# RMSNorm with Silu on one core: from six slots of four rows a partition to three slots of eight

## The chip, the cores and the metric

The kernel runs on one core of a Trainium2 chip. The time is device microseconds of one execution, the median of several runs. Beside it there is a profiled execution, with its span from the first to the last instruction, and a trace that lists instructions and DMA packets. The core's engines are called PE (TensorE, matrix products), DVE (VectorE), ACT (ScalarE), POOL (GpSimd) and SP (SyncE, which here only issues DMAs). Data moves between HBM and the on-chip memory SBUF by 16 DMA engines. SyncE and ScalarE each have a queue of DMAs; both queues are served by the same 16 engines.

## What is computed

The input x has 8 x 1024 rows of 2048 float32 values, 67.1 MB; the output is as large. Each row is divided by its root mean square, multiplied by gamma, and put through Silu.

```python
def reference(x, gamma, eps):
    rms = np.sqrt(np.mean(x ** 2, axis=-1, keepdims=True) + eps)
    out = gamma * x / rms
    return (out * (1 / (1 + np.exp(-out)))).astype(np.float32)
```

## The kernel before

The 8192 rows are cut into 16 blocks of 512. In a block each of the 128 partitions holds J = 4 rows that follow one another in HBM, so that a partition's share is one run of 4 x 8 KB = 32 KB, and a block is 4 MB. A pool has BUFS = 6 slots of one block each (192 KB a partition in all). A block is computed in place and stored from its slot, and then the slot is free for the sixth block after it.

For one block b the steps are:

- `load(b)`: one DMA of the block, issued on ScalarE's queue (L54).
- `squares_scalar(b)` and `squares_vector(b)`: for each row the sum of squares, on ScalarE by an activation Square with an accumulator (L65), on VectorE by a multiply with an accumulator (L73). `share(b)` says how many rows ScalarE takes: two, or one for the even blocks from 4 to 12. What the squares write goes to PSUM tiles `junk_a` and `junk_v` that nobody reads.
- `root(b)`: the square root of the mean plus eps, on ScalarE (L82). It needs another activation table than Silu, so that table loads (ACT_TABLE_LOAD) stand ahead of L82 and L98.
- `invert(b)`: the reciprocal, on VectorE (L87), which gives rstd.
- `multiply(b)`: x times rstd times gamma, row by row in one VectorE instruction with two products (L92). gamma lies in the tile `g`, spread over all partitions at the start by four matrix products with a column of ones (L113) and a copy (L115).
- `silu(b)`: Silu in place, two rows to an instruction, on ScalarE (L98), and then `store(b)`: one DMA of the block, issued on SyncE's queue (L102).

The order is written out by hand (manual_schedule): each engine runs its instructions in the order in which the program text names them, and waits only for the data, buffers and semaphores that an instruction needs. Blocks 0 to 5 are loaded at the start: 0 and 1 first, the other four after gamma's copy. From then on the load of block b + 3 is issued by ScalarE within the squares of block b + 1, behind whatever ScalarE still has to do, and it waits for the store of block b - 3. In the loop over b the steps of blocks b and b + 1 are interleaved in three ways: one for b < SOON = 3, one for the middle, one for the last two. The last block is done differently: its product is with gamma alone (L155), and rstd goes into Silu as a scale, row by row (L157).

Of the kernel before, what the change touches and what calls it, by code (L numbers as in the profile page):

```python
# [1 line left out]

# [4 lines left out]

ACT = mybir.ActivationFunctionType
ALU = mybir.AluOpType


@with_exitstack
def kernel(
    ctx: ExitStack,
    tc: tile.TileContext,
    x: bass.AP,
    gamma: bass.AP,
    eps: bass.AP,
    out: bass.AP,
):  # L20

    nc = tc.nc
    P = nc.NUM_PARTITIONS
    f32 = mybir.dt.float32
    x2 = x.flatten_outer_dims()
    o2 = out.flatten_outer_dims()  # L30
    n, d = x2.shape
    J = 4
    BUFS = 6
    nblk = n // (P * J)
    xb = x2.rearrange("(b p j) d -> b p (j d)", p=P, j=J)
    ob = o2.rearrange("(b p j) d -> b p (j d)", p=P, j=J)

    singles = ctx.enter_context(tc.tile_pool(name="singles", bufs=1))
    pool = ctx.enter_context(tc.tile_pool(name="pool", bufs=BUFS))
    small = ctx.enter_context(tc.tile_pool(name="small", bufs=2))  # L40
    psum = ctx.enter_context(tc.tile_pool(name="psum", bufs=1, space=bass.MemoryType.PSUM))

    Q = 4
    w = d // Q
    g = singles.tile([P, d], f32)
    eps_t = singles.tile([P, 1], f32)
    ones = singles.tile([P, P], f32)
    junk_a = psum.tile([P, d], f32, name="junk_a")
    junk_v = psum.tile([P, d], f32, name="junk_v")
    blocks, sss, rmss, rstds = {}, {}, {}, {}  # L50

    def load(b):
        xt = pool.tile([P, J * d], f32, name="xt")
        nc.scalar.dma_start(out=xt, in_=xb[b])  # L54
        blocks[b] = xt

    def row(b, j):
        return blocks[b][:, j * d:(j + 1) * d]

    def squares_scalar(b, loads=()):  # L60


        sss[b] = small.tile([P, J], f32, name="ss")
        for j in range(share(b)):
            nc.scalar.activation(out=junk_a, in_=row(b, j), func=ACT.Square,  # L65
                                 accum_out=sss[b][:, j:j + 1])
            if j == 0:
                for s in loads:
                    load(s)

    def squares_vector(b):
        for j in range(share(b), J):
            nc.vector.tensor_tensor_reduce(  # L73
                out=junk_v, in0=row(b, j), in1=row(b, j), scale=1.0, scalar=0.0,
                op0=ALU.mult, op1=ALU.add, accum_out=sss[b][:, j:j + 1])

    def share(b):
        return 1 if 4 <= b <= 12 and b % 2 == 0 else 2

    def root(b):  # L80
        rms = small.tile([P, J], f32, name="rms")
        nc.scalar.activation(out=rms, in_=sss.pop(b), func=ACT.Sqrt, scale=1.0 / d, bias=eps_t)  # L82
        rmss[b] = rms

    def invert(b):
        rstd = small.tile([P, J], f32, name="rstd")
        nc.vector.reciprocal(out=rstd, in_=rmss.pop(b))  # L87
        rstds[b] = rstd

    def multiply(b):  # L90
        for j in range(J):
            nc.vector.scalar_tensor_tensor(out=row(b, j), in0=row(b, j), scalar=rstds[b][:, j:j + 1],  # L92
                                           in1=g, op0=ALU.mult, op1=ALU.mult)

    def silu(b):
        for h in range(0, J, 2):
            cols = slice(h * d, (h + 2) * d)
            nc.scalar.activation(out=blocks[b][:, cols], in_=blocks[b][:, cols], func=ACT.Silu)  # L98
        store(b)

    def store(b):
        nc.sync.dma_start(out=ob[b], in_=blocks[b])  # L102

    with tc.manual_schedule():

        load(0)
        nc.vector.memset(ones, 1.0)  # L107
        nc.vector.memset(eps_t, float(eps))
        nc.scalar.activation(out=junk_a[:, 0:1], in_=ones[:, 0:1], func=ACT.Square)  # L109
        nc.sync.dma_start(out=g[0:1, :], in_=bass.AP(tensor=gamma.tensor, offset=gamma.offset, ap=[[d, 1], [1, d]]))  # L110
        for c in range(Q):
            cols = slice(c * w, (c + 1) * w)
            nc.tensor.matmul(junk_v[:, cols], ones[0:1, :], g[0:1, cols], start=True, stop=True)  # L113
        load(1)
        nc.vector.tensor_copy(out=g, in_=junk_v)  # L115
        nc.scalar.copy(out=junk_a[:, 0:1], in_=junk_v[:, d - 1:d])  # L116
        for b in range(2, BUFS):
            load(b)

        last = nblk - 1
        SOON = 3
        squares_scalar(0)
        squares_vector(0)
        root(0)
        invert(0)
        for b in range(last):
            loads = [b + 3] if BUFS <= b + 3 < nblk else []
            if b < SOON:  # L130
                multiply(b)
                squares_scalar(b + 1, loads)
                silu(b)
                squares_vector(b + 1)
                root(b + 1)
            elif b < last - 1:
                squares_scalar(b + 1, loads)
                squares_vector(b + 1)
                root(b + 1)
                multiply(b)  # L140
                silu(b)
            else:
                multiply(b)
                squares_scalar(b + 1)
                silu(b)
                squares_vector(b + 1)
                root(b + 1)
            if b + 1 < last:
                invert(b + 1)


        for j in range(J):
            if j == J // 2:
                invert(last)
            nc.vector.tensor_mul(out=row(last, j), in0=row(last, j), in1=g)  # L155
        for j in range(J):
            nc.scalar.activation(out=row(last, j), in_=row(last, j), func=ACT.Silu,  # L157
                                 scale=rstds[last][:, j:j + 1])
        store(last)


# [1 line left out]
_INS = ['x', 'gamma', 'eps']  # L163
_OUTS = [((8, 1024, 2048), 'float32')]

_NUMBERS = {'eps': 9.999999747378752e-06}


# [26 lines left out]
```

## Time and profile before

| what | value |
|---|---|
| median of 3 runs (lowest, highest) | 316.79 us (316.73, 317.04) |
| span of the profiled execution | 315.1 us |
| moved by DMA, mean rate over the span | 134.24 MB, 426 GB/s |
| DMAs: loads, stores, gamma | 16, 16, 1 |
| one 4096 KB load, median from issue to landing | 38.7 us |
| one 4096 KB store, median from issue to landing | 29.0 us |
| first store issued, last store issued | 35.2 us, 300.9 us |
| VectorE's last instruction starts | 294.2 us |
| ACT_TABLE_LOAD, each | 1283 ns, 31 times |

The page gives the busy time of each engine and how busy the 16 DMA engines are in 40 equal slices of the span. A digit is a tenth, and 9 means 90% or more. A group's line names a line of the kernel, the engine, the operation, the tiles written and read, their shape and the count; then the busy time in all and the mean of one in ns; then the idle time of the engine just before these instructions, and what ended it. A line of the waits names who waited for whom: microseconds in total, the number of times, the longest. The engine's long waits name a DMA or another engine; whether a wait matters depends on what is busy meanwhile.

The trace's packet records go deeper than the page: each packet that a DMA engine moved is listed with its queue, start, duration and bytes. Here a partition's run of 32 KB is one packet, a load is 128 packets, 8 on each of the 16 engines, and a DMA ends on each engine with a packet of 4 bytes that counts up its semaphore.

### The profile page before, as it was taken

The page shows a single profiled execution, that of the slowest core. Times are in us where ns is not written, and L with a number is a line of the kernel's source. Part 1 is how long each engine was busy: PE and PEld are TensorE (multiplying, and loading weights), DVE is VectorE, ACT ScalarE, POOL GpSimd, SP SyncE. Part 2 cuts the span into 40 slices and gives each one's busy share as a digit, 9 for nine tenths or more (in the row PEclk, how much of TensorE's full clock was granted, in tenths as well). Part 3 has the DMA queues.
Part 4 walks back from the last instruction along what each step waited for, and adds up shares of the span by engine and source line. Part 5 has one row for each costly group of instructions (what it writes and reads, how often), then busy time and mean ns, then how long its engine had stood idle before and what let it go on. Part 6 is the DMA issues. An engine that isn't in the chain of part 4 may idle for free.

```text
span 315.1 us, 439 instructions
## 1 busy us (share of the span) xinstructions
PE 7.2 (2%) x8; PEld 2.5 (1%) x8; DVE 235.3 (75%) x157; ACT 213.9 (68%) x137; POOL 0.2 (0%) x4
## 2 busy tenths in 40 slices
PE   6200000000000000000000000000000000000000
PEld 2000000000000000000000000000000000000000
DVE  0679697979895695957969489593995939999600
ACT  1269998972799258682687827877278768779910
POOL 0000000000000000000000000000000000000000
DMA  8999999999999999999999999999999999999997
GB/s 334 412 453 416 383 458 408 462 403 462 403 459 408 454 412 458 408 462 403 462 403 462 408 458 408 458 408 458 416 449 416 449 416 449 428 437 428 437 428 308
DMA packets 4613, 134.24 MB, mean 426 GB/s; under 512 B 514, under 2 KB 514, under 8 KB 514
## 3 DMA queue, kind: packets, MB, share of 16 engines
q10 hardware_dynamic: 2304, 67.11, 49.8%
q1 hardware_dynamic: 2306, 67.12, 49.3%
q14 instruction: 3, 0.02, 0.0%
HBM read 67.12 MB, written 67.11 MB: 426 GB/s over the span
## 4 chain that ended last, share of the span: by engine, by line
DMA 68%; DVE 14%; ACT 11%; issue 1%; ACTq 1%; DVEq 0%
DMA xt<-in_x_dram 68%; DVE xt L92 9%; DVE junk_v L73 5%; ACT xt L98 4%; ACT junk_a L65 3%; ACT xt L157 2%; ACT L82 1%; ACTq L190 1%; ACT L157 0%; ACT L98 0%; ACT rms L82 0%; DVE ss L73 0%; ACTq L54 0%; DVE rstd L87 0%; ACT L109 0%
## 5 line engine op out<-in xcount | busy, mean ns | idle before, releaser
L92 DVE SCALAR_TENSOR_TENSOR xt<-xt,rstd,g 128x2048 f32<-128x2048 f32 x60 | 137.0, 2346 | 0.1
L98 ACT ACTIVATE xt<-xt 128x4096 f32<-128x4096 f32 x30 | 108.3, 3615 | 27.4 <-DVE xt L92 27.4
L73 DVE CUSTOM_DVE_ANT_0 junk_v<-xt 128x2048 f32<-128x2048 f32 x37 | 85.1, 2299 | 42.9 <-DMA xt<-in_x_dram 42.2
L65 ACT ACTIVATE junk_a<-xt 128x2048 f32<-128x2048 f32 x27 | 50.7, 1876 | 16.1 <-DMA xt<-in_x_dram 14.0
L82 ACT ACT_TABLE_LOAD x15 | 19.2, 1283 | 26.6 <-DVE ss L73 26.5
L98 ACT ACT_TABLE_LOAD x14 | 18.0, 1283 | 0.2
L115 DVE COPY g<-junk_v 128x2048 f32<-128x2048 f32 x1 | 2.3, 2292 | 9.0 <-PE junk_v L113 9.0
L87 DVE RECIPROCAL rstd<-rms 128x4 f32<-128x4 f32 x16 | 2.7, 172 | 8.4 <-ACT rms L82 8.4
L155 DVE TENSOR_TENSOR xt<-xt,g 128x2048 f32<-128x2048 f32 x4 | 8.9, 2277 | 0.0
L82 ACT ACTIVATE rms<-ss,eps_t 128x4 f32<-128x4 f32 x16 | 4.8, 297 | 5.7 <-DVE ss L73 5.5
L157 ACT ACTIVATE xt<-xt,rstd 128x2048 f32<-128x2048 f32 x4 | 7.7, 1991 | 0.0
L113 PE MATMUL junk_v<-g,ones 1*128 1x512 f32 x8 | 7.2, 1072 | 2.8 <-DMA g<-in_gamma_dram 2.8
L116 ACT COPY junk_a<-junk_v 128x1 f32<-128x1 f32 x1 | 0.1, 144 | 9.8 <-DVE g L115 9.8
L73 DVE DVE_READ_ACCUMULATOR2_ANT ss<- 128x1 f32 x37 | 5.2, 141 | 0.0
L65 ACT ACTIVATION_READ_ACCUMULATOR junk_a<-xt 128x1 f32 x27 | 5.0, 186 | 0.0
L113 PEld LDWEIGHTS junk_v<-g,ones 1*128 1x128 f32 x8 | 2.5, 325 | 5.9 <-issue 5.9
L109 ACT ACT_TABLE_LOAD x1 | 1.3, 1283 | 1.1 <-PEq L176 1.1
L157 ACT ACT_TABLE_LOAD x1 | 1.3, 1283 | 0.0
L107 DVE MEMSET ones<- 128x128 f32 x1 | 0.2, 165 | 0.8 <-PEq L176 0.8
L109 ACT ACTIVATE junk_a<-ones 128x1 f32<-128x1 f32 x1 | 0.2, 174 | 0.0
L176 POOL MEMSET const-bfloat16-1.0<- 128x1 bf16 x1 | 0.1, 103 | 0.0
L176 POOL MEMSET const-uint8-127<- 128x1 uint8 x1 | 0.1, 102 | 0.0
(3 smaller groups left out, 0.3 us busy)
## 6 DMA issues: line engine op xcount, KB each, us to landing
xt<-in_x_dram ACTq DMA_DIRECT2D x16, 4096.0 KB, 38.7
out_dram<-xt SPq DMA_DIRECT2D x16, 4096.0 KB, 29.0
g<-in_gamma_dram SPq DMA_DIRECT2D x1, 8.0 KB
```

Source lines behind the costliest of these rows:

```text
L65: nc.scalar.activation(out=junk_a, in_=row(b, j), func=ACT.Square, accum_out=sss[b][:, j:j + 1])
L73: nc.vector.tensor_tensor_reduce(out=junk_v, in0=row(b, j), in1=row(b, j), scale=1.0, scalar=0.0, op0=ALU.mult, op1=ALU.add, accum_out=sss ...
L82: nc.scalar.activation(out=rms, in_=sss.pop(b), func=ACT.Sqrt, scale=1.0 / d, bias=eps_t)
L87: nc.vector.reciprocal(out=rstd, in_=rmss.pop(b))
L92: nc.vector.scalar_tensor_tensor(out=row(b, j), in0=row(b, j), scalar=rstds[b][:, j:j + 1], in1=g, op0=ALU.mult, op1=ALU.mult)
L98: nc.scalar.activation(out=blocks[b][:, cols], in_=blocks[b][:, cols], func=ACT.Silu)
L109: nc.scalar.activation(out=junk_a[:, 0:1], in_=ones[:, 0:1], func=ACT.Square)
L113: nc.tensor.matmul(junk_v[:, cols], ones[0:1, :], g[0:1, cols], start=True, stop=True)
L115: nc.vector.tensor_copy(out=g, in_=junk_v)
L155: nc.vector.tensor_mul(out=row(last, j), in0=row(last, j), in1=g)
L157: nc.scalar.activation(out=row(last, j), in_=row(last, j), func=ACT.Silu, scale=rstds[last][:, j:j + 1])
L190: with _tile.TileContext(nc) as tc:
```

## The change

- The table FILLINGS replaces J and BUFS. The pool has three slots of eight rows a partition (64 KB). A filling says which blocks a slot holds and how many rows a store takes. The first and the last filling are two blocks of four rows each, loaded and stored one by one; the six between them are one block of eight rows, one 8 MB load with runs of 64 KB. Five of these six are stored by one DMA, the last of them by two of four rows.
- Loads are issued on SyncE, stores and gamma's load on ScalarE.
- Each block is computed as a whole by `compute(b)`, with no interleaving of two blocks: half of the rows' squares on VectorE, half on ScalarE; the root; then VectorE multiplies every row by gamma alone, with the reciprocal behind the first product; then Silu row by row with rstd as its scale. A store is issued right behind the last Silu that it covers.
- The small tiles have three buffers in place of two. The loads of a slot's next filling stand behind the compute of its present one in the program, on SyncE, where only loads are queued.
- The activation that read gamma's copy (L116) is gone, and all loads of the three slots are issued at once.

```diff
+FILLINGS = [
+    [(4, 4), (4, 4)],
+    [(8, 8)],
+    [(8, 8)],
+    [(8, 8)],
+    [(8, 8)],
+    [(8, 8)],
+    [(8, 4)],
+    [(4, 4), (4, 4)],
+]
+SLOTS = 3
...
-    pool = ctx.enter_context(tc.tile_pool(name="pool", bufs=BUFS))
-    small = ctx.enter_context(tc.tile_pool(name="small", bufs=2))
+    pool = ctx.enter_context(tc.tile_pool(name="pool", bufs=SLOTS))
+    small = ctx.enter_context(tc.tile_pool(name="small", bufs=3))
...
+    def load(b, slot):
+        b.slot = slot
+        nc.sync.dma_start(out=rows(b, 0, b.rows), in_=b.x)
+
+    def fill(k):
+        slot = pool.tile([P, ROWS * d], f32, name="xt")
+        for b in fillings[k]:
+            load(b, slot)
+
+    def rows(b, j, k=1):
+        return b.slot[:, (b.offset + j) * d:(b.offset + j + k) * d]
+
+    def compute(b):
+        J = b.rows
+        half = J // 2
+        ss = small.tile([P, ROWS], f32, name="ss")
+        rms = small.tile([P, ROWS], f32, name="rms")
+        rstd = small.tile([P, ROWS], f32, name="rstd")
+        for j in range(half):
+            nc.vector.tensor_tensor_reduce(
+                out=junk_v, in0=rows(b, j), in1=rows(b, j), scale=1.0, scalar=0.0,
+                op0=ALU.mult, op1=ALU.add, accum_out=ss[:, j:j + 1])
+        for j in range(half, J):
+            nc.scalar.activation(out=junk_a, in_=rows(b, j), func=ACT.Square,
+                                 accum_out=ss[:, j:j + 1])
+        nc.scalar.activation(out=rms[:, 0:J], in_=ss[:, 0:J], func=ACT.Sqrt, scale=1.0 / d, bias=eps_t)
+        for j in range(J):
+            nc.vector.tensor_mul(out=rows(b, j), in0=rows(b, j), in1=g)
+            if j == 0:
+                nc.vector.reciprocal(out=rstd[:, 0:J], in_=rms[:, 0:J])
+        for j in range(J):
+            nc.scalar.activation(out=rows(b, j), in_=rows(b, j), func=ACT.Silu,
+                                 scale=rstd[:, j:j + 1])
+            k = b.per_store
+            if (j + 1) % k == 0:
+                first = j + 1 - k
+                nc.scalar.dma_start(out=b.out[:, first * d:(j + 1) * d], in_=rows(b, first, k))
...
+        slot = pool.tile([P, ROWS * d], f32, name="xt")
+        load(fillings[0][0], slot)
...
+        for b in fillings[0][1:]:
+            load(b, slot)
         nc.vector.tensor_copy(out=g, in_=junk_v)
...
+        for k in range(1, SLOTS):
+            fill(k)
+        for k in range(len(fillings)):
+            for b in fillings[k]:
+                compute(b)
+            if k + SLOTS < len(fillings):
+                fill(k + SLOTS)
```

## The prediction

> **What bounds the kernel now.** I read the page's first three parts first, to see which resource is never free, then the waits, then stretches of time, then the records of single DMA packets.
>
> ```profile
> span 315.1 us, 439 instructions
> PE 7.2 (2%) x8; PEld 2.5 (1%) x8; DVE 235.3 (75%) x157; ACT 213.9 (68%) x137; POOL 0.2 (0%) x4
> DMA  8999999999999999999999999999999999999997
> DMA packets 4613, 134.24 MB, mean 426 GB/s; under 512 B 514, under 2 KB 514, under 8 KB 514
> q10 hardware_dynamic: 2304, 67.11, 49.8%
> q1 hardware_dynamic: 2306, 67.12, 49.3%
> ```
>
> VectorE and ScalarE are idle a quarter and a third of the span. The DMA engines are at nine tenths or more in all slices but the ends, and their two queues (q10 carries the loads, q1 the stores) take 99.1% of 16 engines' span. The waits agree: VectorE's and ScalarE's longest are for data.
>
> ```profile
> DVE junk_v L73 <- DMA xt<-in_x_dram: 42.2, 11, 5.7
> ACT xt L98 <- DVE xt L92: 27.4, 23, 2.8
> ```
>
> The stretches of time tell whether the DMA engines ever lose time (columns: start and end, length, busy of PE, PEld, DVE, ACT and POOL, clock, DMA share, GB/s).
>
> ```profile
> 35.00:60.00 25.00, 0.00 (x0) 0.00 (x0) 21.40 (x14) 23.19 (x18) 0.00 (x0) 1.00 1.00 418
> 60.00:300.00 240.00, 0.00 (x0) 0.00 (x0) 192.76 (x128) 170.37 (x105) 0.00 (x0) 1.00 1.00 433
> ```
>
> From 60 us on the rate is flat at 433 GB/s. Around 36 us, where the first store enters, it sags. The packet records (start, duration and bytes of each packet) say it exactly. An engine moves 256 packets of 32 KB, one every 1.2097 us, loads and stores strictly by turns while both queues hold work; a DMA's end costs 6 ns (its 4-byte semaphore packet), and no engine is ever without a packet from 1.77 to 313.1–314.0 us. The loss against that beat comes to 0.54 us an engine in the first packets and 0.88 us an engine at 36.2 to 38.4 us, when 31 load packets take 1.29 to 2.06 us in place of 1.213, just ahead of the first store packet at 39.6 us. The remaining excess is under 0.1 us an engine. So the time is bytes over DMA rate, plus ends. A faster VectorE or ScalarE buys nothing; the change can gain per packet and can lose where engines stall or run dry.
>
> **The change, part by part.** The sum is made on the profiled execution: its span of 315.1 us; the median of the three runs, 316.79, lies 1.7 us above, for what surrounds the span.
>
> Packets. Six loads and five stores move eight rows a partition, so 11 x 8 = 88 packets of 64 KB an engine replace 176 of 32 KB; bytes stay. What a packet costs beyond its bytes is shown by no row, so I bound it. From below: nothing (or 64 KB runs are cut in two). From above: 6 ns, what a packet of 4 bytes takes. Between them stands the 8 KB instruction packet that lengthened one engine's step at 107.6 us to 1515 ns: 1515 - 1209.7 = 305.3 ns for 8 KB, and a line through it and 1209.7 for 32 KB has a fixed part of (4 x 305.3 - 1209.7) / 3 = 3.8 ns. I take it: 88 x 3.8 = 0.33 us saved, ends 0 and 0.53.
>
> DMAs. 33 become 22 (10 loads, 11 stores, gamma): 11 x 6 ns = 0.07 us saved. The Trainium skill ("SBUF — State Buffer", The DMA setup-cost knee) says that every transfer pays a roughly fixed 2 us and advises coalescing; by that rule 11 fewer would save 22 us. The trace's engines pass from one DMA to the next in 6 ns, so the fixed part lies under the DMA queued behind.
>
> Compute. The multiply turns from L92's form into that of L155, squares are split evenly, Silu takes single rows with a scale, and table loads fall from 31 to 21.
>
> ```profile
> L92 DVE SCALAR_TENSOR_TENSOR xt<-xt,rstd,g 128x2048 f32<-128x2048 f32 x60 | 137.0, 2346 | 0.1
> L73 DVE CUSTOM_DVE_ANT_0 junk_v<-xt 128x2048 f32<-128x2048 f32 x37 | 85.1, 2299 | 42.9 <-DMA xt<-in_x_dram 42.2
> L155 DVE TENSOR_TENSOR xt<-xt,g 128x2048 f32<-128x2048 f32 x4 | 8.9, 2277 | 0.0
> L157 ACT ACTIVATE xt<-xt,rstd 128x2048 f32<-128x2048 f32 x4 | 7.7, 1991 | 0.0
> ```
>
> In the timeline two squares with their accumulator reads start 2.39 us apart, and two products take 4.49, so 2.25 each. An eight-row block from landing to its store: 4 x 2.39 + 8 x 2.25 + 0.17 (reciprocal) + 1.99 (the last Silu, which waits for the last product) = 29.7 us; ScalarE's 4 x 2.03 + 1.28 + 0.30 + 1.28 + 8 x 1.92 = 26.3 us lies beside that. A four-row block: 4.8 + 9.0 + 0.2 + 2.0 = 16.0 us. The DMA needs 32 x 1.21 = 38.7 us for load and store of eight rows, so compute is hidden with 9 us to spare a fill: cost nothing, and without that cover each microsecond over 38.7 would count once a fill. A store issue on ScalarE (0.33 us, behind the last Silu) delays only the squares behind it, inside the same slack.
>
> Queues. Loads on SyncE wait for a slot's stores alone; nothing else is queued behind them. In before a load sat behind ScalarE's work (issued at 66.7, though its slot's store left the engine at 57.9).
>
> Slots. Three slots turn in 3 x 38.7 = 116.1 us. A slot needs a load at half rate (38.7), compute (29.7), a store at half rate (38.7), and twice about 1.9 us from one DMA's end to the next one's first packet (engines end up to 0.9 us apart, and 1.03 us passes from issue, at 0.73 us, to the first packet): 110.9. So 5 us are left. Playing the turns forward: the first store is issued at about 28.4 us (35.2 before); then each 64 KB load packet and 32 KB store packet take 3.63 us a pair. Fill 1 is in at 45, its store issued at 75.6; the load queue is empty at 75; the last store of fill 0 ends at 79.1, and the load that waits for it brings packets at about 80.6. Fill 1's store has work from 76.6, so engines stay fed, with 2.5 us to spare. From then on a store ends one packet (2.42 us) before the running load, and the next load arrives 1.9 us after it: 0.5 us before the load queue is dry. At the end three four-row stores (24 packets, 29.0 us) are left when the last load is in; the last must arrive within 16 packets, 19.4 us, and does after 0.9 + 16.0 + 1.0 = 17.9.
>
> Restart of an empty queue. At 80.6 us a queue that has been empty for 5 us gets work while the other runs. The trace has one such event, the first store, at 0.88 us; the other end is 0.02 us, for the four loads appended at 12.4 us to a queue that still held work. Being empty, ours is nearest the first: 0.88 us lost. The first store's own stall stays in both kernels.
>
> Sum: -0.33 - 0.07 + 0.88 = +0.48 us: span 315.6, time 317.3 us. The measurement tells about 0.2% from no change, 0.63 us, so this is no change.
>
> Runs of 64 KB put partitions 64 KB apart in HBM. The Trainium skill ("DMA: Bandwidth & Descriptors", Latency and other measured facts) warns of large power-of-two row pitches: 207 GB/s a direction at 512 KiB, against 214 in full. If 64 KB already cost that 3.4%, 11/16 of 309.7 us would grow by 7.2 us. At a pitch of 32 KB this trace shows packets of 1.213 us throughout; no row here shows 64 KB.
>
> **Rivals.**
>
> 1. Slower: restarts again and again. Price 0.88 each; the place is the load queue at about 117, 156, 195 and 234 us. It decides once a store's end to the next load's arrival takes over 2.42 us, or if an engine that reads ahead finds the queue empty a packet early. For it: a margin of only 0.5 us. Against: appending to a queue in work cost 0.02 us. All five: 316.79 - 0.40 + 4.4 = 320.8 us; two: 318.2.
> 2. Faster: the 36 us stall belongs to that one moment, and neither it nor the restart is paid: 316.79 - 0.40 - 0.88 = 315.5 us. For it: single event, cause unseen. Against: after too opens its stores beneath a full load queue. A stall of its present size with a free restart gives 316.4, still no change.
> 3. The runs are cut into 32 KB packets: 316.79 - 0.07 + 0.88 = 317.6 us. For it: nothing longer is in the trace; against: before's 32 KB runs went as one packet.
> 4. Packets of 64 KB run below the beat, by HBM or the engine's buffer: 1% on 213 us is +2.1, 319.4 us with the rest. Against: 3928 of 4096 packets took 1213 ns, loads and stores, alone or by turns, so something fixed in the engine sets the rate.
>
> **How the numbers follow.** Forecast or free restart, both within 0.2%: 0.44. Rival 1: 0.27; rival 2: 0.20; rival 3: 0.03; rival 4: 0.06. Faster 0.20, same 0.44, slower 0.27 + 0.03 + 0.06 = 0.36. The forecast's own range is 316.2 (6 ns a packet, restart free) to 317.4. Most chance beyond lies on the slow side; the whole range takes in rival 1 up to three or four restarts and rival 2 nearly to its full size: 315.7 to 319.5 us.
>
> **What would show it.** Right: packets of 65536 bytes about every 2.416 us; loads and stores by turns; one patch of stretched packets near 30 us and one near 81 us, none later; engines without a gap to the end; first store at about 28 us. Wrong: stretched packets or gaps once a fill (rival 1), a beat above 2.42 us (rival 4), 32 KB packets (rival 3), no patch at 81 us (cheaper than I say), or a gap before the last store near 301 us.

## The result and the profile after

The changed kernel takes 321.68 us (median of 5, 320.0 to 322.18), the kernel before 317.02 us (median of 5, 316.73 to 317.16) beside it: a ratio of 1.0134 with a 95% interval of 1.0119 to 1.015. It is 1.3% slower. The forecast was 317.3 us and no change, in a range up to 319.5.

The page of the changed kernel, its span, the 40 slices and the DMA part:

```profile
span 320.4 us, 412 instructions
PE 7.2 (2%) x8; PEld 2.5 (1%) x8; DVE 218.9 (68%) x141; ACT 219.9 (69%) x160; POOL 0.2 (0%) x4
DMA  8999889899999999999999999999999999999766
GB/s 328 450 401 524 385 360 499 376 409 458 467 451 393 425 483 393 393 515 401 393 507 401 393 499 409 393 499 417 393 450 462 393 405 438 442 413 454 344 275 270
DMA packets 3029, 134.25 MB, mean 419 GB/s; under 512 B 337, under 2 KB 337, under 8 KB 337
```

The bytes are the same, the packets a third fewer. What is new is the end: the last three slices stand at 7, 6 and 6 tenths, where before only the very last one fell, to 7. Before, the DMA engines worked to the end; here they stop and start again.

The waits and the costliest groups of the changed kernel, against those of the prediction:

```profile
DVE junk_v L91 <- DMA xt<-in_x_dram: 74.3, 9, 21.0
ACT xt L103 <- DVE xt L99: 4.6, 22, 0.4
```

```profile
L99 DVE TENSOR_TENSOR xt<-xt,g 128x2048 f32<-128x2048 f32 x64 | 142.2, 2278 | 0.0
L103 ACT ACTIVATE xt<-xt,rstd 128x2048 f32<-128x2048 f32 x64 | 125.7, 1997 | 5.4 <-DVE xt L99 4.6
L91 DVE CUSTOM_DVE_ANT_0 junk_v<-xt 128x2048 f32<-128x2048 f32 x32 | 73.6, 2299 | 75.0 <-DMA xt<-in_x_dram 74.3
```

The compute engines wait for each other less (ScalarE for VectorE 4.6 us, 27.4 before) and longer for data (74.3 us, 42.2 before): the loss is not in compute. The stretches of time place it (columns: start and end, length, busy of PE, PEld, DVE, ACT and POOL, clock, DMA share, GB/s):

```profile
80.00:240.00 160.00, 0.00 (x0) 0.00 (x0) 104.97 (x66) 104.06 (x74) 0.00 (x0) 1.00 1.00 432
240.00:282.00 42.00, 0.00 (x0) 0.00 (x0) 36.73 (x25) 35.51 (x28) 0.00 (x0) 1.00 1.00 431
282.00:303.00 21.00, 0.00 (x0) 0.00 (x0) 15.15 (x11) 16.27 (x13) 0.00 (x0) 1.00 0.99 426
303.00:308.00 5.00, 0.00 (x0) 0.00 (x0) 2.23 (x2) 4.19 (x3) 0.00 (x0) 1.00 0.11 46
308.00:319.00 11.00, 0.00 (x0) 0.00 (x0) 0.00 (x0) 0.00 (x0) 0.00 (x0) 1.00 0.90 385
```

Up to 303 us the rate is close to the kernel before's 433 GB/s: 426 to 432. Then for 5 us almost nothing moves. The kernel before in the same two last stretches:

```profile
303.00:308.00 5.00, 0.00 (x0) 0.00 (x0) 0.00 (x0) 0.00 (x0) 0.00 (x0) 1.00 0.99 426
308.00:319.00 11.00, 0.00 (x0) 0.00 (x0) 0.00 (x0) 0.00 (x0) 0.00 (x0) 1.00 0.44 191
```

The timeline of the changed kernel's end says what the DMA engines wait for:

```profile
287.92 0.34 ACTq L108 DMA_DIRECT2D out_dram<-xt  x1
291.67 1.88 ACT L95 ACTIVATE junk_a<-xt 128x2048 f32<-128x2048 f32 x1 [3.78 <-DMA xt<-in_x_dram]
291.67 2.30 DVE L91 CUSTOM_DVE_ANT_0 junk_v<-xt 128x2048 f32<-128x2048 f32 x1 [5.82 <-DMA xt<-in_x_dram]
...
307.30 0.34 ACTq L108 DMA_DIRECT2D out_dram<-xt  x1
```

VectorE and ScalarE wait for the last load until 291.67 us, compute it in 15.6 us, and the last store is issued at 307.30 us. Yet the packet records show that 13 of the 16 DMA engines had moved their part of that load by 281.7 us, two more by 286.4, and the last one only by 290.1. A load has landed when its slowest engine is done, and that engine was 8 to 9 us behind most of the others. (A record doesn't name its engine; a packet is put down to the engine whose last packet ends where it starts, so that engines whose packets end together can be taken for each other.) Read out of the packet records, for both kernels (a stretched packet is one over 25 ns longer than its size's usual time, counted after 45 us, summed over the engines):

```
         stretched packets   last load packet ends   last packet ends     idle at the end
         number, us          first .. last engine    first .. last        engines, us each
before       3    0.5          276.8 .. 277.6          313.1 .. 314.0       0
changed     65   12.2          280.0 .. 290.1          317.9 .. 319.1      15, 2.4 to 5.3
```

The engine furthest behind has 6.2 of the 12.2 us of stretched packets. It is the one without idle time, and it ends last, at 319.1 us; the 15 that stood idle end at 317.9 to 318.6. Of the 12.2 us, 8.6 lie in load packets and 3.6 in store packets.

So there are two things to explain: why a few engines fall behind on stretched packets, and how that turns into idle time on all the others. The packets themselves are cheaper, as forecast: where nothing is stretched, the next packet follows a 64 KB one after 2414.3 ns, and two of 32 KB took 2418.9.

### The profile page after: what moved, and what is told of

The parts are those of the page before. It is cut to its first block, busy times and chain, and to the rows that moved or that the text cites. A ratio compares the mean times of both kernels' runs of the same rounds, so it can differ in the third digit from the quotient of the medians.

```text
span 320.4 us, 412 instructions
## 1 busy us (share of the span) xinstructions
PE 7.2 (2%) x8; PEld 2.5 (1%) x8; DVE 218.9 (68%) x141; ACT 219.9 (69%) x160; POOL 0.2 (0%) x4
## 4 chain that ended last, share of the span: by engine, by line
DMA 66%; DVE 25%; ACT 2%; another core or an unknown queue 2%; SPq 0%; issue 0%; DVEq 0%
DMA xt<-in_x_dram 39%; DMA out_dram<-xt 27%; DVE xt L99 16%; DVE junk_v L91 9%; ACT xt L103 2%; SPq L74 0%; DVE ss L91 0%; DVE rstd L101 0%; DVEq L160 0%
## 5 line engine op out<-in xcount | busy, mean ns | idle before, releaser
L99 DVE TENSOR_TENSOR xt<-xt,g 128x2048 f32<-128x2048 f32 x64 | 142.2, 2278 | 0.0
L103 ACT ACTIVATE xt<-xt,rstd 128x2048 f32<-128x2048 f32 x64 | 125.7, 1997 | 5.4 <-DVE xt L99 4.6
L91 DVE CUSTOM_DVE_ANT_0 junk_v<-xt 128x2048 f32<-128x2048 f32 x32 | 73.6, 2299 | 75.0 <-DMA xt<-in_x_dram 74.3
L95 ACT ACTIVATE junk_a<-xt 128x2048 f32<-128x2048 f32 x32 | 60.2, 1881 | 69.3 <-DMA xt<-in_x_dram 67.8
L95 ACT ACTIVATION_READ_ACCUMULATOR junk_a<-xt 128x1 f32 x32 | 6.0, 186 | 0.0
L91 DVE DVE_READ_ACCUMULATOR2_ANT ss<- 128x1 f32 x32 | 4.5, 140 | 0.0
L97 ACT ACTIVATE rms<-ss,eps_t 128x8 f32<-128x8 f32 (+1 forms) x10 | 3.0, 299 | 0.1
L101 DVE RECIPROCAL rstd<-rms 128x8 f32<-128x8 f32 (+1 forms) x10 | 1.9, 186 | 1.4 <-ACT rms L97 1.4
L116 ACT ACTIVATE junk_a<-ones 128x1 f32<-128x1 f32 x1 | 0.2, 174 | 0.0
```

The costliest lines, as they stand in the source:

```text
L91: nc.vector.tensor_tensor_reduce(out=junk_v, in0=rows(b, j), in1=rows(b, j), scale=1.0, scalar=0.0, op0=ALU.mult, op1=ALU.add, accum_out=s ...
L95: nc.scalar.activation(out=junk_a, in_=rows(b, j), func=ACT.Square, accum_out=ss[:, j:j + 1])
L97: nc.scalar.activation(out=rms[:, 0:J], in_=ss[:, 0:J], func=ACT.Sqrt, scale=1.0 / d, bias=eps_t)
L99: nc.vector.tensor_mul(out=rows(b, j), in0=rows(b, j), in1=g)
L101: nc.vector.reciprocal(out=rstd[:, 0:J], in_=rms[:, 0:J])
L103: nc.scalar.activation(out=rows(b, j), in_=rows(b, j), func=ACT.Silu, scale=rstd[:, j:j + 1])
```

## The experiments

Three theories were put against each other first. P: the 64 KB packet gets stretched. Y: partitions 64 KB apart in HBM collide. S: three slots and loads on SyncE let engines drift.

**Both directions in 32 KB packets, at the changed layout.**

```diff
-        nc.sync.dma_start(out=rows(b, 0, b.rows), in_=b.x)
+        for r in range(0, b.rows, 4):
+            nc.sync.dma_start(out=rows(b, r, 4), in_=b.x[:, r * d:(r + 4) * d])
...
-                nc.scalar.dma_start(out=b.out[:, first * d:(j + 1) * d], in_=rows(b, first, k))
+                for r in range(first, j + 1, 4):
+                    nc.scalar.dma_start(out=b.out[:, r * d:(r + 4) * d], in_=rows(b, r, 4))
```

> The changed kernel with each 8-row load and store as two DMAs of four rows: same slots, same block layout (a partition's rows still 64 KB apart from the next one's), same order, but packets of 32 KB. In the changed kernel's trace three of the 16 engines fall up to 9 us behind on stretched load packets, and the last store waits for them. Theory P (the 64 KB packet is what gets stretched once an engine is out of step): no engine lags by over 1 us when the last load ends, time 316.5 to 317.5 us. Theory Y (runs that lie 64 KB apart in HBM collide): the lag stays, 320 to 322 us. Theory S (three slots, loads on SyncE: the structure lets engines drift): the lag stays, 320 to 322 us.

Measured: 318.61 us, ratio 1.0055 [1.0039, 1.0071]; the last load ends 275.9 to 279.4 us over the engines, none idle afterwards. Between P and the others. Of 16.7 us of stretched packets 15.6 lie in one patch at 120 to 140 us, on all engines, 1.0 us each on average (0.3 to 1.7), where the load queue had run dry and starts again. Apart from that patch hardly anything is stretched (1.1 us over 16 engines), so layout alone does not do it.

**Only the loads in 32 KB packets** (the first half of that diff).

> Only the loads in two DMAs of four rows (packets of 32 KB); stores keep packets of 64 KB. Nearly all stretched packets were loads. Theory P, in the form that long load packets are at fault: no lag, and 40 store packets an engine still save 5 ns each, 316.3 to 317.3 us. If long packets of either kind are enough: 318 to 321 us. Theories Y and S: 320 to 322 us.

Measured: 330.13 us, ratio 1.0397 [1.036, 1.0433], worse than anything expected; 113.9 us of stretched packets. The two queues are served packet by packet in turn, so that 32 KB loads beside 64 KB stores get a third of the bytes (from 84 to 92 us, 1.05 MB of loads and 2.29 MB of stores); the loads fall behind, and the store queue runs dry once a fill. But stretched packets also stand where both queues simply alternate.

**Only the stores in 32 KB packets** (the second half).

> Only the stores in two DMAs of four rows; loads keep packets of 64 KB. Theory P with long load packets at fault: the lag stays, 319 to 322 us. If it takes long stores beside long loads: no lag, 316.3 to 317.3 us. Theories Y and S: 320 to 322 us.

Measured: 317.43 us, ratio 1.0019 [1.001, 1.0029]; 4.4 us of stretched packets, last loads 277.5 to 278.6 us. Beside stores of 32 KB, loads of 64 KB are harmless; it is the stores. The stretches of time of this kernel, for the end that was idle above:

```profile
282.00:303.00 21.00, 0.00 (x0) 0.00 (x0) 11.75 (x9) 12.87 (x11) 0.00 (x0) 1.00 1.00 430
303.00:308.00 5.00, 0.00 (x0) 0.00 (x0) 0.00 (x0) 0.00 (x0) 0.00 (x0) 1.00 0.97 419
```

From 303 to 308 us the engines now move 419 GB/s, where they moved 46; VectorE and ScalarE have long finished.

**Three slots with blocks of four rows throughout.**

```diff
-    [(8, 8)],
-    [(8, 8)],
-    [(8, 8)],
-    [(8, 8)],
-    [(8, 8)],
-    [(8, 4)],
+    [(4, 4), (4, 4)],
+    [(4, 4), (4, 4)],
+    [(4, 4), (4, 4)],
+    [(4, 4), (4, 4)],
+    [(4, 4), (4, 4)],
+    [(4, 4), (4, 4)],
```

> Three slots and the changed kernel's queues and compute, but every slot holds two blocks of four rows: packets of 32 KB, runs 32 KB apart, as before the change. Theories P and Y: no engine lags, 316.5 to 317.5 us. Theory S: the lag stays, 320 to 322 us.

Measured: 317.39 us, ratio 1.0019 [1.001, 1.0028]; 2.8 us of stretched packets. The three slots, the queues and the new compute cost 0.6 us together (0.3 to 0.9), and S falls. Of its engines 14 are done by 313.8 us; the last one, at 314.5, moved two of the three instruction packets. These are packets of 8 KB that the page lists as `q14 instruction`; they go over the same 16 DMA engines.

**A shorter tail.**

```diff
-    [(4, 4), (4, 4)],
+    [(4, 4), (2, 2), (2, 2)],
 ]
```

> The changed kernel with its last filling cut into blocks of 4, 2 and 2 rows, so that the last store is issued some 7 us sooner after the last load lands. In the changed kernel 15 engines stood idle 2.4 to 5.3 us at 303 to 308 us waiting for that store, and one engine without any idle time ended at 317.9 us. Theory late store (the idle time is the loss; engines' lag matters only through it): 316.5 to 318 us. Theory lag (the engine that fell furthest behind sets the end by itself): the idle stretch goes, but the time falls by 1.5 us at most, to 319.5 to 322 us.

Measured: 321.03 us, ratio 1.0123 [1.0086, 1.016]. The idle stretch does not go, though it shrinks: 12 engines, 2.3 to 3.1 us each, between 308 and 312 us:

```profile
303.00:308.00 5.00, 0.00 (x0) 0.00 (x0) 4.97 (x5) 4.52 (x6) 0.00 (x0) 1.00 0.89 382
308.00:319.00 11.00, 0.00 (x0) 0.00 (x0) 0.12 (x1) 2.41 (x2) 0.00 (x0) 1.00 0.57 241
```

Those are the shortened tail's last stretches; the second, at 241 GB/s in place of 385, holds the wait. In this run the engines lag more (22.6 us stretched; the furthest ends its last load at 299.6 us, most at 291 to 292), and that engine ends at 319.0 us without any idle time. So the lag itself is the loss; the late store is how the other engines come to share it. The same holds for the changed kernel, where the engine without idle time ended at 319.1 us (317.9, in the expectation, is the end of the others).

**The changed kernel once more**, with nothing edited.

> The changed kernel once more, for a second profile. Theory fetch (an 8 KB instruction packet puts an engine out of step, and from then on its 64 KB packets are stretched): the engines that lag are again those that move an instruction packet before 250 us. Theory chance (any engine may fall out of step): the lagging engines are others. 320 to 322.5 us by both.

Measured: 321.55 us, in a single run. Three engines lag again, by 5.5, 2.3 and 2.1 us of stretched packets. Two of them moved an instruction packet (85.5 and 90.3 us), as two of the three did in the first profile. The third did not, in either profile.

**More instruction packets, in both kernels.**

```diff
+        pad = singles.tile([P, 1], f32, name="pad")
+        for _ in range(1536):
+            nc.gpsimd.memset(pad, 0.0)
```

> The changed kernel with 1536 tiny memsets on GpSimd, which nothing waits for: they add some 12 instruction packets of 8 KB, 0.3 us each on one engine or another. Theory fetch: each one puts an engine out of step, so more stretched packets, and the time rises well beyond the packets' own time, to 323 us or more. Theory chance: at most the packets' own time, up to 12 x 0.3 = 3.7 us if all fall on the last engine, and less if they spread: 320 to 324 us with no growth of the stretched packets' total (12 us over the 16 engines after 45 us).

> The kernel before the change with the same 1536 memsets on GpSimd. Theory fetch: packets of 32 KB are not stretched after a fetch, so the time rises by no more than the packets' own 0.3 us each on the engine that moves them: 317 to 320.6 us, and the stretched packets outside the fetch itself stay under 2 us over all engines. If fetches hurt 32 KB packets as much: 323 us or more.

Measured: the changed kernel 326.03 us, ratio 1.0272 [1.0235, 1.0308], 70.9 us of stretched packets, a growth that theory fetch asks for. But all 12 packets for GpSimd went over one DMA engine, and the other 15 have 3.6 to 6.1 us of stretched packets each, most of them without an instruction packet: that is not what the theory says. The kernel before takes 322.38 us, 1.0174 [1.0155, 1.0194], with 5.2 us. It was expected at 320.6 us at most, with under 2 us of stretched packets, and shows something by itself. Here too the 12 packets went over one DMA engine, which ended its last load at 284.0 us, the others at 276 to 278.5. The slices of the DMA engines on the page of this second run:

```profile
DMA  8999999999999999999999999999999999997996
```

And its end by stretches of time:

```profile
282.00:303.00 21.00, 0.00 (x0) 0.00 (x0) 20.92 (x13) 19.05 (x12) 0.00 (x0) 1.00 0.86 368
303.00:308.00 5.00, 0.00 (x0) 0.00 (x0) 0.00 (x0) 4.36 (x3) 0.00 (x0) 1.00 0.75 321
308.00:319.00 11.00, 0.00 (x0) 0.00 (x0) 0.00 (x0) 0.00 (x0) 0.00 (x0) 1.00 0.90 384
```

Here the kernel before, with 32 KB packets, has a dip like the changed kernel's, at 282 to 308 us. Delaying one engine of 16 is enough: its load lands late, the compute and the stores behind it come late, and 14 of the other engines idle for 2.9 to 3.3 us at a stretch.

**Instruction packets moved to the start.** In the changed kernel, with short stores, and in the kernel before:

```diff
+        early_v = singles.tile([P, 52], f32, name="early_v")
+        early_a = singles.tile([P, 56], f32, name="early_a")
+        for c in range(52):
+            nc.vector.memset(early_v[:, c:c + 1], 0.0)
+        for c in range(56):
+            nc.scalar.copy(out=early_a[:, c:c + 1], in_=ones[:, 0:1])
```

> The changed kernel with 52 tiny memsets on VectorE and 56 tiny copies on ScalarE in the first 13 us, when both engines wait anyway. The two instruction packets of 85 and 90 us came when ScalarE had run 64 of its instructions and VectorE some 53; they now come in the first 13 us, while only 32 KB loads run, and ScalarE's next one near 240 us, VectorE's near 290 us. Theory fetch: nearly no stretched packet from 80 to 235 us, the furthest engine is at most 3 us behind at the last load (8 to 9 before), 317 to 319.5 us. Theory chance (engines fall out of step without a fetch): 320 to 322.5 us as before.

> The same, with stores in two DMAs of four rows (64 KB load packets, 32 KB store packets), which took 317.4 us without the early instructions. Theory fetch: 0.3 to 0.7 us less, since the slowest engine was one that moved two instruction packets: 316.6 to 317.2 us. Theory chance: 317.2 to 317.8 us.

> The kernel before the change with the same early instructions. Its engines with an instruction packet lagged by 0.24 to 0.36 us alone, so little is to be had: 316.4 to 317.1 us by both theories; over 317.5 us would mean that the early instructions cost something themselves.

Measured: 321.75 us (1.0151 [1.0138, 1.0164]), 318.87 us (1.0061 [1.0049, 1.0074]) and 317.61 us (1.0022 [1.0013, 1.0031]). The packets did move, to 17 and 18 us, and later ones came at 219 and 259 us in the first. Theory fetch falls: between 80 and 235 us the changed kernel still has some 13 us of stretched packets, now spread over most engines, and 27 us more from 240 to 280 us, where 64 KB stores run beside 32 KB loads. Its stretch there:

```profile
240.00:282.00 42.00, 0.00 (x0) 0.00 (x0) 37.17 (x25) 35.95 (x28) 0.00 (x0) 1.00 1.00 416
```

That is 416 GB/s where the changed kernel without the early instructions moved 431. More fetches came with more stretched packets, but engines fall out of step without one. The other two kernels missed their forecasts, the last by passing 317.5 us, which stood for a cost of the early instructions themselves. Their next instruction packets came at 210 and 269, and at 226 and 234 us, each on an engine that had moved an early one: the two engines with two packets ended at 314.7 and 315.6, and at 314.3 and 314.9 us, all the others by 313.7 and 313.5.

**Is it the packet or the 8 MB store, and how long may a packet be?** Stores as two DMAs of even and odd partitions (64 KB packets in 4 MB DMAs), and as two DMAs of six and two rows (48 KB and 16 KB packets):

```diff
+                for r in ((0, 1) if k == 8 else (None,)):
+                    sel = slice(r, P, 2) if r is not None else slice(0, P)
+                    nc.scalar.dma_start(out=b.out[sel, first * d:(j + 1) * d], in_=rows(b, first, k)[sel, :])
```
```diff
+                for lo, hi in (((first, first + 6), (first + 6, first + 8)) if k == 8 else ((first, j + 1),)):
+                    nc.scalar.dma_start(out=b.out[:, lo * d:hi * d], in_=rows(b, lo, hi - lo))
```

> The changed kernel with each eight-row store as two DMAs over the even and the odd partitions: as many store DMAs of 4 MB as with stores in halves of four rows (317.4 us), but the packets stay at 64 KB. Theory length (the 64 KB store packet is what gets engines out of step and stretched): 320 to 323 us, some 10 us or more of stretched packets over the engines. Theory size (it is the 8 MB store, one landing for eight rows): 317 to 318.5 us.

> The changed kernel with each eight-row store as two DMAs of six and two rows, packets of 48 and 16 KB. Theory length, if the harm grows with the packet: between 317.4 (32 KB) and 321.7 us (64 KB), about 318 to 320.5 us. If only 64 KB does harm, as at a limit of some buffer: 317 to 318 us.

Measured: 329.5 us (1.0372 [1.0314, 1.043]) with 101.2 us of stretched packets, and 317.73 us (1.0028 [1.0016, 1.0039]) with 2.2 us. Halving the store's size and leaving its packets at 64 KB does not help; shortening the packets to 48 KB does. The middle of the first, by stretches of time:

```profile
80.00:240.00 160.00, 0.00 (x0) 0.00 (x0) 105.05 (x66) 105.06 (x76) 0.00 (x0) 1.00 1.00 418
```

Its engines are busy (a share of 1.00) and move 418 GB/s where the changed kernel moves 432: that is what stretched packets look like in a mean. The order of partitions within a store differs in the first, so that its 8 us over the changed kernel are not explained; that the 4 MB size does not cure is. In the second, 14 of 16 engines finish between 312.6 and 313.3 us, where the kernel before's finish between 313.1 and 314.0; the last, at 314.6, moved an instruction packet. The second kernel's rate over the middle, and its end:

```profile
80.00:240.00 160.00, 0.00 (x0) 0.00 (x0) 110.77 (x71) 109.94 (x81) 0.00 (x0) 1.00 1.00 434
...
303.00:308.00 5.00, 0.00 (x0) 0.00 (x0) 0.00 (x0) 0.00 (x0) 0.00 (x0) 1.00 1.03 446
```

No version ran faster than the kernel before.

## Why the prediction was wrong

- **The bound** was right. Between 80 and 240 us the changed kernel moves 432 GB/s, about as before (433 from 60 to 300 us). A mean over 16 engines hides what one of them loses.
- **Packets.** The fixed part was put at 3.8 ns and measured 2418.9 - 2414.3 = 4.6 ns; 88 of them are 0.40 us in place of 0.33, within the ends given. The earlier end of most engines in the kernel with 48 KB stores fits that gain.
- **DMAs.** An engine still passes from one DMA to the next in 6 ns.
- **Compute** was right: the first store was issued at 28.65 us (28.4 forecast), fill 1's at 77.06 (75.6), and from the last load's landing to the last store there were 15.6 us (16.0).
- **First store's stall** stayed: at 31.4 to 31.9 us 16 load packets of 64 KB took 3.2 to 3.4 us in place of 2.418, on average 0.88 us each.
- **Restart of the load queue at 81 us**: it came at 85.4 us. A loss of 0.88 us was forecast, and it cost nothing on most engines with no instruction packet nearby (load packets of 2418 ns from the start). It is not always free: in the first experiment such a restart cost 1.0 us, at 125 to 137 us. Rival 1, which would have repeated it each fill, names times near the result (318.2 to 320.8), but not what happened: the loss came in no patches common to all engines once a fill.
- **The spread of the engines is the step that failed.** The sum has one loss or gain for all 16 engines alike and none for a single engine; the tail was worked out with the 0.9 us between the first and the last engine of the kernel before, as if that were fixed. In the changed kernel the last load ended 8.6 us later on one engine than on most. That engine had 6.2 us of stretched packets and no idle time, and ended at 319.1 us, where the last engine before ended at 314.0: these 5.1 us are nearly all of the 5.3 us between the two profiled spans.
- **The tail** went wrong by the same step. When most engines had moved their last load, at 281.5 us, their queues held stores until 303.2, or 21.7 us (19.4 forecast). The last store's packets came after 8.6 (spread) + 1.5 (to the start of compute) + 15.6 + 0.9 = 26.6 us (17.9 forecast), so that most engines were idle for some 5 us. More room here would not have saved the time, since the engine that ended last was never idle; the shorter tail of the fifth experiment, at 321.03 us, agrees.
- **Runs 64 KB apart in HBM** did not cost the 7.2 us that were reckoned with as a possibility: with this layout and shorter store packets the first and third experiments took 318.61 and 317.43 us.
- **Rival 4** had the right place, 64 KB packets taking longer, at 0.06 and as a rate common to all. The beat is intact on most engines; a few engines lose it and never make it up. The argument against it, that 3928 of 4096 packets took 1213 ns whatever ran beside them, held for 32 KB alone.

Two parts are shown: 64 KB store packets bring the loss (48 KB and 32 KB ones do not, with loads, layout, slots and compute alike), and one late engine holds up all the others. Why a 64 KB store packet makes this engine or that one lose time is open; layout alone, the load packet's length, the store's size and instruction packets are ruled out as the whole of it.

## What to carry to other kernels

When the DMA engines are the bound, look at each of them, not at their mean: a load lands with its slowest engine, and an engine without idle time never catches up. The spread of the engines measured in one kernel need not hold in a kernel with other packets. More room at the tail keeps the other engines busy, but does not give back what the slowest one has lost. Longer packets gained about 5 ns each here and were safe for loads of 64 KB beside stores of up to 48 KB; stores of 64 KB cost ten times the gain.

## What was not expected of the hardware

- Two queues are served packet by packet, not byte by byte: 32 KB loads beside 64 KB stores got a third of the rate, and the kernel took 330.13 us.
- By the counts, an instruction packet of 8 KB comes when an engine has run about 64 of its instructions, and again at about 192 (in the changed kernel ScalarE had 62 and 67 recorded at the first two packets and 192 at the third; a record doesn't say for which engine a packet is). It takes 0.3 us of one DMA engine, often with 0.3 to 0.6 us more in the packet behind it. In the two kernels with early instructions and store packets of 32 KB, the engines that moved two ended at 314.3 to 315.6 us, all the others by 313.7.
